# A hybrid encoder layer on Trainium2: left operands of the FFN's second Strassen half on GpSimd's queue, splits issued in two parts, RG-LRU's splits in an earlier slot

## The chip, the cores and the metric

The kernel runs on one core of one Trainium2 chip. The metric is the device time of one execution in microseconds (us), as the median of several runs.

## The reference

One encoder layer for two groups of tokens, a prompt of 1024 and a sample of 512, with shared weights and D = 1024; all arithmetic is float32. Cut to what matters:

```
h   = rmsnorm(x) * (1 + sc1) + sh1
z   = h @ w_in                       # rnn_x, rnn_gate, q, k, v, merge gates
xc  = conv4(rnn_x)
r,i = sigmoid(xc @ wa + ba), sigmoid(xc @ wx + bx)      # 16 blocks of 64, two directions
a   = exp(-8 r softplus(-lam));  u = sqrt(1 - a*a) * i * xc
rec = scan_forward(a, u) + scan_backward(a, u)          # RG-LRU
x   = x + gt1 * (merge(rec * gelu(gate), attention(q, k, v)) @ w_out)
h2  = rmsnorm(x) * (1 + sc2) + sh2
ff  = (silu(h2 @ w_g) * (h2 @ w_u)) @ w_ffn_out         # w_ffn_out: 2816 x 1024
y   = rmsnorm(x + gt2 * ff) * final_g
```

## The kernel before, in words

Every float32 product is made of three matmuls: an operand is split into a first part (rounded to the matmul's type, a ScalarE cast) and a second part (what is left, a VectorE subtraction), and first x first, first x second and second x first are added in PSUM. The helper `split` (L148 to L150) does cast and subtraction one behind the other. The order of all work is written out by hand: each engine runs its instructions in program order, DMA queues included, and only data and buffers make one engine wait for another.

**RG-LRU** (140 to 530 us). For each of eight column blocks j, TensorE makes one tile of `rnn_x` and one of the gate, each in six half groups of 12 matmuls of 512 columns. After every half group one slot of side work is taken from a list. `first` puts the six gates of a block (`gate`, L527 to L535: six matmuls into two of the four PSUM banks of the pool `sd`, then two ScalarE sigmoids that free them) into six slots; `second` (L600) puts the rest there: `exps` (X), the convolution of the next block (C), the two decays (E, three VectorE operations each), the split of the next block's `xc` (CS, L518 and L519), the split of its gate weights (`gw_split`, L499 and L500), the roots (Q, L558 and L559, two ScalarE operations each, of which one needs the decay), a scan (S) and Gelu (GE).

**FFN, second Strassen half** (from 2521 us). `w_ffn_out` is cut into 2 x 2 blocks, and seven products replace eight. Each product has six left operands (pairs of 128-token tiles), so there are 42 steps n. A step is 11 slices k of three matmuls with 512 columns (`mms`, L1600 to L1604), first parts first; even steps write the PSUM tile `mm` and read `a0hi`, `a0lo`, odd ones `sd` and `a1hi`, `a1lo`.

- `aload(n)` (L1285 to L1299) loads the left operand of step n, 128 x 1408 float32 or 704 KB, from `ffd` or `ffx` into one of two raw buffers (`araw`, seen as `slot` for even n and `wol` for odd); in two of the products it loads two of them. It is an SP DMA.
- `aprep(n, i)` (L1301) prepares part i of three of it: where there are two operands a VectorE sum (L1315, `asum`), then `split` into `acmb`. Two such pairs exist, so the parts of step n + 2 may be written only when TensorE is done with the same part of step n.
- `bbuild` (L1265) makes the right operand's slices for the next product, 11 in six steps: one or two loads of 256 KB from `w_fo` (`bload`, L1263, SP, two raw buffers `wo`; the load for slice n + 2 waits until slice n is split), a VectorE sum or difference (L1274) where there are two, and `split`.
- `take` (L1570) adds the finished product to the accumulators `acc` (L1526), `x1load` (L1534, SP) fetches the residual, `squares` (L1540, L1541 and L1543) adds it and sums the squares.

In the loop over the steps (L1625) the helpers stand at fixed slices k:

```python
if k == 1 and n: aprep(n + 1, 2); aload(n + 2)
elif k == 2: take(n - 1), x1load
elif k in (3, 6): bbuild(...)
elif k == 4: aprep(n + 2, 0)
elif k == 8: aprep(n + 2, 1)
elif k == 9 and done: squares(...)
```

Of the kernel before, what the change touches and what calls it, by code (L numbers as in the profile page):

```python
# [14 lines left out]
ALU = mybir.AluOpType  # L15
# [8 lines left out]
CH = 512  # L24
# [27 lines left out]
def encoder_kernel(  # L52
# [5 lines left out]
    v, s, g_, pe, sp = nc.vector, nc.scalar, nc.gpsimd, nc.tensor, nc.sync  # L58
# [55 lines left out]
    class Stream:  # L114
# [13 lines left out]
        def split(self, n, eng=v):  # L128
            self.load(n)
            while self.ns < min(n, len(self.srcs)):  # L130
                t = self.raws.pop(self.ns)
                hi = self.pool.tile(self.shape, F32R, tag=self.tags[1], name="whi")
                lo = self.pool.tile(self.shape, F32R, tag=self.tags[2], name="wlo")
                split(t, hi, lo, eng)
                self.parts[self.ns] = (hi, lo)
                self.ns += 1
# [299 lines left out]
    with ExitStack() as sc:  # L436
# [58 lines left out]
        def gw_split(j):  # L495
            a = graw.pop(j)
            for b, h in enumerate(hs):
                hi, lo = (w[h, :, 64 * b:64 * b + 64] for w in gws[j % 2])
                s.copy(out=hi, in_=a[h])  # L499
                v.tensor_tensor(out=lo, in0=a[h], in1=hi.bitcast(F32), op=ALU.subtract)  # L500
# [85 lines left out]
        def slots(*fs):  # L586

            for f in fs:
                side.append(lambda f=f: [a() for a in f])
# [10 lines left out]
        def second(p, c, j):  # L600

            C, CS = ([c["C"]], [c["CS"]]) if c else ([], [])
            gs = [lambda: gw_split(j)] if c else []
            if p:
                slots([p["X"]] + C + [p["E"][0]], [p["E"][1]], CS + [p["Q"][0]], gs + [p["Q"][1]], [p["S"][0]], [p["GE"]])
            else:
                slots(C, gs, CS, [], [], [])

# [5 lines left out]
        p = pp = None  # L614
        for j in range(KD):
# [9 lines left out]
            p, pp = cur, p  # L625
# [495 lines left out]
    def f32(a):  # L1121
        return a.bitcast(F32)
# [110 lines left out]
    KH = NFF // 2  # L1233
    AH = KH * P
# [14 lines left out]
    araw = [f32(slot[i][:, :2 * AH]) for i in (4, 3)]  # L1249
# [4 lines left out]
    def bload(upto):  # L1254

        while nbl[0] < min(upto, len(PRODO) * KH):
            q, k = divmod(nbl[0], KH)
            t = braw[nbl[0]] = wts.tile([P, D], F32, tag="raw", name="wo2")
            nbl[0] += 1
            for e, nm in enumerate(PRODO[q][2][:2]):  # L1260
                if nm:
                    i, j = int(nm[0]) - 1, int(nm[1]) - 1
                    sp.dma_start(out=t[:, e * CH:(e + 1) * CH], in_=w_fo[KH * i + k, :, j * CH:(j + 1) * CH])  # L1263

    def bbuild(upto):  # L1265

        while nbb[0] < min(upto, len(PRODO) * KH):
            n = nbb[0]
            bload(n + 1)
            nbb[0] += 1  # L1270
            t, r = braw.pop(n), bslot[n % 20]
            op = PRODO[n // KH][2][2]
            if op is not None:
                v.tensor_tensor(out=t[:, :CH], in0=t[:, :CH], in1=t[:, CH:], op=op)  # L1274
            split(t[:, :CH], r[:, :CH], r[:, CH:])
            bload(n + 3)

    def asrc(nm, i):
        t = PAIRS[i]
        if nm in ("d0", "d1", "s"):  # L1280
            return ffx[i, {"d0": 0, "d1": 1, "s": 2}[nm]]
        b = int(nm[1]) - 1
        return ffd[t + (3 if nm[0] == "2" else 0), :, b * AH:(b + 1) * AH]

    def aload(n):  # L1285

        if n >= NSTEP:
            return
        q, i = divmod(n, len(PAIRS))
        if n == 0:  # L1290
            a0["raw"] = upper
            for nm in ("hi", "lo"):
                a0[nm] = [wts.tile([P, D], F32R, tag=nm, name="a0" + nm) for _ in range(2)]
            bslot.extend(a0["hi"] + a0["lo"])
            for e, (o, w) in enumerate(((0, D), (D, AH - D))):
                sp.dma_start(out=a0["raw"][e][:, :w], in_=asrc("11", 0)[:, o:o + w])
            return
        for e, nm in enumerate(PRODO[q][1]):
            sp.dma_start(out=araw[n % 2][:, e * AH:(e + 1) * AH], in_=asrc(nm, i))  # L1299

    def aprep(n, i):  # L1301

        if n >= NSTEP:
            return
        c = slice(CH * i, min(CH * (i + 1), AH))
        w = c.stop - c.start
        if n == 0:
            e, o = divmod(CH * i, D)
            split(*(a0[nm][e][:, o:o + w] for nm in ("raw", "hi", "lo")))
            return  # L1310
        a, (hi, lo) = araw[n % 2], acmb[n % 2]
        t = a[:, c]
        if len(PRODO[n // len(PAIRS)][1]) == 2:
            t = tmp.tile([P, CH], F32, tag="t2", name="asum")[:, :w]
            v.tensor_tensor(out=t, in0=a[:, c], in1=a[:, AH + c.start:AH + c.stop], op=ALU.add)  # L1315
        split(t, hi[:, c], lo[:, c])

    def apart(n, k):
        if n:
# [4 lines left out]
    def column(p):  # L1324

        return p % NFF // 2 + NFF // 2 * (p % 2)
# [60 lines left out]
    with ExitStack() as sc:  # L1387
# [54 lines left out]
        for m, (p, c) in enumerate(order):  # L1442
# [3 lines left out]
            X, Y, u2, r = TX[p % 2], TX[2 + p % 2], TX[4 + p % 2], TX[6 + p % 2]  # L1446
            i, t0 = column(p), p // NFF * 6
# [65 lines left out]
    with ExitStack() as sc:  # L1513
# [16 lines left out]
        def x1load(t, f):  # L1530
            e, m = divmod(nx[0] % 4, 2)
            nx[0] += 1
            a = upper[e][:, m * CH:(m + 1) * CH]
            sp.dma_start(out=a, in_=x1d[t * P:(t + 1) * P, f])  # L1534
            return a

        def squares(t, f, xo, ps):

            a = acc[t][:, f]
            v.tensor_tensor(out=a, in0=a, in1=gt2[t // 8][:, f], op=ALU.mult)  # L1540
            v.tensor_tensor(out=a, in0=a, in1=xo, op=ALU.add)  # L1541
            e = f.start // CH
            s.activation(out=ps, in_=a, func=AF.Square, accum_out=st[:, 2 * t + e:2 * t + e + 1])  # L1543
# [56 lines left out]
        def mms(ps, n, k, cols=slice(0, CH)):  # L1600
            hi, lo, bh, bl = operands(n, k)
            pe.matmul(ps, lhsT=hi, rhs=bh[:, cols], start=k == 0, stop=False)
            pe.matmul(ps, lhsT=hi, rhs=bl[:, cols], start=False, stop=False)
            pe.matmul(ps, lhsT=lo, rhs=bh[:, cols], start=False, stop=k == KH - 1)  # L1604
# [4 lines left out]
        for n, k, f in (  # L1609
# [7 lines left out]
        ):  # L1617
            late[n, k] = f

        ps = None  # L1620
        tl = PAIRS[-1]
        for i in range(3):
            aprep(1, i)
        aload(2)
        for n in range(NSTEP - 1):  # L1625
            q, i = divmod(n, len(PAIRS))
            before, ps = ps, (sdb if n % 2 else mmb)()
            done = xo = None
            for k in range(KH):
                mms(ps, n, k)  # L1630
                if k == 1 and n:
                    aprep(n + 1, 2)
                    aload(n + 2)
                elif k == 2:
                    if n:
                        done = take(n - 1, before)
                    if q == 3 or done and done[1] is F2 and done[0] in PAIRS:
                        done = (PAIRS[i], F2) if q == 3 else None
                    if done:
                        xo = x1load(*done)  # L1640
                elif k in (3, 6):
                    t = (q + 1) * KH + (2, 4, 6, 8, 9, 11)[i]
                    bbuild(t - 1 if k == 3 else t)
                elif k == 4:
                    aprep(n + 2, 0)
                elif k == 8:
                    aprep(n + 2, 1)
                    if n == 0:
                        sp.dma_start(out=fgb, in_=final_g.partition_broadcast(P))
                        for e in range(2):  # L1650
                            src = gtd[1, e:e + 1, :].partition_broadcast(P)
                            sp.dma_start(out=gt2[e], in_=src.rearrange("p a d -> p (a d)"))
                elif k == 9 and done:
                    squares(*done, xo, before)
                if (n, k) in late:
                    late[n, k]()
            if n == NSTEP - 3:
                xl = x1load(tl, F1)
            if n == NSTEP - 2:

                a = acc[tl]
                v.tensor_tensor(out=a[:, F1], in0=a[:, F1], in1=gt2[1][:, F1], op=ALU.mult)
                v.tensor_tensor(out=a[:, F1], in0=a[:, F1], in1=xl, op=ALU.add)
                v.tensor_tensor(out=a[:, F2], in0=a[:, F2], in1=fgb[:, F2], op=ALU.mult)

        n = NSTEP - 1
        b = wts.tile([P, CH], F32, tag="raw", name="b")
        for e, pl in enumerate((sdb(), mmb())):
            cols = slice(256 * e, 256 * e + 256)
            pl = pl[:, cols]  # L1670
            for k in range(KH):
                mms(pl, n, k, cols)
                if e == 0 and k == 1:
                    late[n, 0]()
                    done = take(n - 1, ps)
# [11 lines left out]
            if e == 0:  # L1687
                v.tensor_tensor(out=st[:, 2 * tl:2 * tl + 1], in0=st[:, 60:61], in1=st[:, 2 * tl + 1:2 * tl + 2],
                                op=ALU.add)
# [3 lines left out]
        r = rs[:, tl:tl + 1]  # L1693
# [90 lines left out]
```

## Time and profile before

| | us |
|---|---|
| median of 3 runs | 2963.2 (2961.89 to 2963.86) |
| the profiled execution | 2960.41 |
| its span in the trace | 2958.6 |
| TensorE matmuls busy | 2832.6 (96%) |
| TensorE weight loads busy | 2351.5 (79%) |
| VectorE busy | 1927.5 (65%) |
| ScalarE busy | 1217.0 (41%) |
| GpSimd busy | 238.0 (8%) |

Engines are named PE (matmuls), PEld (weight loads), DVE (VectorE), ACT (ScalarE), POOL (GpSimd) and SP. L with a number is a line of the kernel before. The times of the rows are microseconds from the start of the span, and matmuls overlap: one of 512 columns is shown as 0.39 us, while the next starts 0.23 us after it. What follows "<-" in brackets is what ended the idle time before an instruction.

### The profile page before, as it was taken

How to read it: one execution, taken by the hardware profiler on the slowest of the kernel's cores; microseconds unless marked ns; L12 is line 12 of the kernel's file. 1: busy time of each engine (PE TensorE's matmuls, PEld its weight loads, DVE VectorE, ACT ScalarE, POOL GpSimd, SP SyncE). 2: the span in 40 equal slices, each digit the busy share in tenths (PEclk: the TensorE clock that was granted, in tenths of full speed). 3: DMA queues.
4: the chain of work that ended last, by engine and by line, in shares of the span. 5: the costliest groups of instructions: out<-in, count | busy, mean ns of one | idle time of the engine just before them, and what ended most of it. 6: DMA issues, size and time to landing. Idle time of an engine off the chain costs nothing. (4 is left out here: it accounts for less than half of the span.)

```text
span 2958.6 us, 38256 instructions
## 1 busy us (share of the span) xinstructions
PE 2832.6 (96%) x14165; PEld 2351.5 (79%) x14165; DVE 1927.5 (65%) x3615; ACT 1217.0 (41%) x2384; POOL 238.0 (8%) x312
## 2 busy tenths in 40 slices
PE   8999999999999999999999999999999999879887
PEld 5878777877777777777787777999999999667665
DVE  6486867455555555542758656898889887456667
ACT  6375757233333333335330145544444443333332
POOL 0000000000000000001523412011000000000001
PEclk9999999999999999999999999999999999899998
DMA  5211011110111011112677644675454443655555
GB/s 231 72 35 57 32 65 55 61 33 33 33 34 40 33 33 34 34 47 65 196 252 254 214 151 136 201 209 171 132 172 128 117 121 119 214 187 196 185 191 183
DMA packets 184395, 351.55 MB, mean 119 GB/s; under 512 B 20264, under 2 KB 99496, under 8 KB 183952
## 3 DMA queue, kind: packets, MB, share of 16 engines
q1 hardware_dynamic: 167648, 292.42, 30.8%
q0 software_dynamic: 16416, 56.42, 5.5%
q8 instruction: 111, 1.82, 0.3%
q14 instruction: 76, 0.62, 0.1%
q10 hardware_dynamic: 144, 0.26, 0.0%
HBM read 264.19 MB, written 84.85 MB: 118 GB/s over the span
## 5 line engine op out<-in xcount | busy, mean ns | idle before, releaser
L159 PE MATMUL mm<-hh,whi 128*128 128x512 f32 x1632 | 664.2, 407 | 2.0 <-DVE hh L292 1.5
L161 PE MATMUL mm<-hh,wlo 128*128 128x512 f32 x1632 | 642.4, 394 | 0.0
L160 PE MATMUL mm<-hl,whi 128*128 128x512 f32 x1632 | 641.5, 393 | 0.5 <-DVE hl L293 0.4
L159 PEld LDWEIGHTS mm<-hh,whi 128*128 128x128 f32 x1632 | 312.3, 191 | 71.1 <-issue 7.2
L161 PEld LDWEIGHTS mm<-hh,wlo 128*128 128x128 f32 x1632 | 308.7, 189 | 68.8
L160 PEld LDWEIGHTS mm<-hl,whi 128*128 128x128 f32 x1632 | 309.8, 190 | 62.8 <-DVE hl L293 3.3
L150 DVE TENSOR_TENSOR wlo<-wraw,whi 128x1024 fp32r<-128x1024 f32 x94 | 115.0, 1229 | 193.2 <-ACT whi L149 193.1
L747 ACT ACTIVATE sm<-sm,sg 128x192 f32<-128x192 f32 (+2 forms) x288 | 114.3, 398 | 303.5 <-DVE sg L742 303.0
L149 ACT CAST whi<-wraw 128x1024 fp32r<-128x1024 f32 x96 | 96.3, 1006 | 198.2 <-PE mm L160 86.2
L1361 DVE TENSOR_TENSOR sum<-wf 128x512 f32<-128x512 f32 x220 | 158.4, 720 | 1.5
L1363 ACT CAST woh<-sum 128x512 fp32r<-128x512 f32 x148 | 91.9, 622 | 153.2 <-DVE sum L1361 149.8
L742 DVE CUSTOM_DVE_ANT_0 sm<-sd,mk 128x192 f32<-128x192 f32 (+2 forms) x288 | 72.9, 291 | 117.0 <-PE sd L735 64.3
L668 DVE SCALAR_TENSOR_TENSOR t<-mm,rp 128x512 f32<-128x512 f32 x72 | 49.8, 692 | 150.3 <-PE mm L161 150.3
L1432 PE MATMUL mm<-top,woh 128*128 128x384 f32 x348 | 116.6, 335 | 3.2 <-DVE flat L1465 3.2
L1434 PE MATMUL mm<-top,woh 128*128 128x384 f32 x348 | 116.3, 334 | 0.0
L1433 PE MATMUL mm<-top,woh 128*128 128x384 f32 x348 | 116.3, 334 | 0.0
L1345 DVE TENSOR_TENSOR woh<-sum,woh 128x512 fp32r<-128x512 f32 x148 | 101.2, 684 | 0.6 <-ACT woh L1363 0.5
L857 DVE CUSTOM_DVE_ANT_0 jk<-ada 128x1024 bf16<-128x1024 f32 x64 | 81.4, 1285 | 22.8 <-DMA ada<-in_w_ada_dram 14.3
L1568 POOL DMA_DIRECT2D out_dram<-acc x22 | 12.0, 545 | 896.4 <-DVE acc L1567 895.0
L1434 PE MATMUL sd<-top,woh 128*128 128x384 f32 x240 | 80.2, 334 | 0.0
L1432 PE MATMUL sd<-top,woh 128*128 128x384 f32 x240 | 80.2, 334 | 0.0
L1433 PE MATMUL sd<-top,woh 128*128 128x384 f32 x240 | 80.2, 334 | 0.0
(446 smaller groups left out, 6465.4 us busy)
## 6 DMA issues: line engine op xcount, KB each, us to landing
wf<-in_w_fi_dram SPq DMA_DIRECT2D x88, 512.0 KB, 3.8
wraw<-in_w_in_dram SPq DMA_DIRECT2D x68, 512.0 KB, 3.5
wo<-in_w_fo_dram SPq DMA_DIRECT2D x132, 256.0 KB, 3.2
ffd<-flat SPq DMA_DIRECT2D x88, 192.0 KB, 3.7
ada<-in_w_ada_dram SPq DMA_DIRECT2D x32, 512.0 KB, 4.2
ffx<-flat SPq DMA_DIRECT2D x66, 192.0 KB, 2.5
wol<-ffd SPq DMA_DIRECT2D x18, 704.0 KB, 4.9
gated<-gs POOLq DMA_DIRECT2D x48, 256.0 KB, 2.6
```

What stands on the lines that cost most here:

```text
L149: s.copy(out=hi, in_=t)
L150: eng.tensor_tensor(out=lo, in0=t, in1=hi.bitcast(F32), op=ALU.subtract)
L159: pe.matmul(ps, lhsT=hi(k), rhs=xh(k), start=a, stop=False)
L160: pe.matmul(ps, lhsT=hi(k), rhs=xl(k), start=False, stop=False)
L161: pe.matmul(ps, lhsT=lo(k), rhs=xh(k), start=False, stop=z)
L747: s.activation(out=sm[:, c], in_=sm[:, c], func=AF.Exp, scale=-1.0, bias=sg[:, u, x:x + 1], accum_out=sg[:, u, x + 1:x + 2])
L1345: v.tensor_tensor(out=r[:, CH:], in0=t, in1=f32(r[:, :CH]), op=ALU.subtract)
L1361: v.tensor_tensor(out=t, in0=wraws[p, a], in1=wraws[p, b], op=op)
L1363: s.copy(out=r[:, :CH], in_=t)
L1432: pe.matmul(ps, lhsT=hi, rhs=bh[:, k], start=k == 0 and not more, stop=False, skip_group_check=more)
L1433: pe.matmul(ps, lhsT=hi, rhs=bl[:, k], start=False, stop=False, skip_group_check=more)
L1434: pe.matmul(ps, lhsT=lo, rhs=bh[:, k], start=False, stop=k == 3, skip_group_check=more)
```

## The change

Three things are moved; no arithmetic is added or taken away.

1. `aload` is issued on GpSimd's queue (except for step 0), and a step earlier: `aload(n + 3)` in step n behind slice 1, when the last part of step n + 1 has been split, which now stands behind slice 0.
2. `bbuild` and `aprep` take a list. With it they issue only the cast, and append the subtraction (with the next `bload`) to the list; the loop issues what is in the list at later slices (`flush`). Slices for `take`, `bbuild` and the second `aprep` are one earlier.
3. In RG-LRU's `second`, the splits of `xc` and the gate weights come ahead of the second decay.

```diff
             if p:
-                slots([p["X"]] + C + [p["E"][0]], [p["E"][1]], CS + [p["Q"][0]], gs + [p["Q"][1]], [p["S"][0]], [p["GE"]])
+                slots([p["X"]] + C + [p["E"][0]], CS + gs + [p["Q"][0]], [p["E"][1]], [p["Q"][1]], [p["S"][0]], [p["GE"]])
...
-            split(t[:, :CH], r[:, :CH], r[:, CH:])
-            bload(n + 3)
+            s.copy(out=r[:, :CH], in_=t[:, :CH])
+
+            def low(n=n, t=t, r=r):
+                v.tensor_tensor(out=r[:, CH:], in0=t[:, :CH], in1=f32(r[:, :CH]), op=ALU.subtract)
+                bload(n + 3)
+            if later is None:
+                low()
+            else:
+                later.append(low)
...
-            sp.dma_start(out=araw[n % 2][:, e * AH:(e + 1) * AH], in_=asrc(nm, i))
+            g_.dma_start(out=araw[n % 2][:, e * AH:(e + 1) * AH], in_=asrc(nm, i))
...
-        split(t, hi[:, c], lo[:, c])
+        s.copy(out=hi[:, c], in_=t)
+
+        def low():
+            v.tensor_tensor(out=lo[:, c], in0=t, in1=f32(hi[:, c]), op=ALU.subtract)
+        if later is None:
+            low()
+        else:
+            later.append(low)
...
+        lows = []
+
+        def flush(fs=None):
+            for f in list(lows if fs is None else fs):
+                lows.remove(f)
+                f()
+
         ps = None
         tl = PAIRS[-1]
+        aload(2)
         for i in range(3):
-            aprep(1, i)
-        aload(2)
+            aprep(1, i, lows)
+            if i:
+                flush(lows[:1])
+        flush()
...
                 mms(ps, n, k)
-                if k == 1 and n:
-                    aprep(n + 1, 2)
-                    aload(n + 2)
-                elif k == 2:
+                if k == 0 and n:
+                    aprep(n + 1, 2, lows)
+                elif k == 1:
                     if n:
                         done = take(n - 1, before)
...
+                    flush()
+                    aload(n + 3)
+                elif k in (2, 5):
+                    t = (q + 1) * KH + (2, 4, 6, 8, 9, 11)[i]
+                    had = list(lows)
+                    bbuild(t - 1 if k == 2 else t, lows)
+                    flush(had)
                 elif k in (3, 6):
-                    t = (q + 1) * KH + (2, 4, 6, 8, 9, 11)[i]
-                    bbuild(t - 1 if k == 3 else t)
+                    flush()
                 elif k == 4:
-                    aprep(n + 2, 0)
-                elif k == 8:
-                    aprep(n + 2, 1)
+                    aprep(n + 2, 0, lows)
+                elif k == 7:
+                    aprep(n + 2, 1, lows)
...
-                elif k == 9 and done:
-                    squares(*done, xo, before)
+                elif k == 9:
+                    flush()
+                    if done:
+                        squares(*done, xo, before)
```

How this moves instructions, at three places. First, SP's queue around step 21 of the FFN's second half, before (`wo` are the right operand's raw buffers, `wol` and `slot` with `ffx` the left operand's, with `x1d` the residual's):

```order
L1263 DMA wo_20813<-in_w_fo_dram 128x512 x2
L1263 DMA wo_20830<-in_w_fo_dram 128x512 x2
L1299 DMA wol<-ffx 128x1408
L1534 DMA slot<-x1d 128x512
L1263 DMA wo_20872<-in_w_fo_dram 128x512 x2
L1263 DMA wo_20889<-in_w_fo_dram 128x512 x2
```

and after the change:

```order
L1263 DMA wo_20814<-in_w_fo_dram 128x512 x2
L1263 DMA wo_20831<-in_w_fo_dram 128x512 x2
L1548 DMA slot<-x1d 128x512
L1263 DMA wo_20873<-in_w_fo_dram 128x512 x2
L1263 DMA wo_20890<-in_w_fo_dram 128x512 x2
```

The left operand's load is gone from between the right operand's loads. On GpSimd's queue these loads now follow one another with nothing between them until the output's stores.

Second, VectorE in step 21, before (L1526 is `take`, L150 the second part of a split, L1274 the right operand's sum, L1540 and L1541 `squares`):

```order
L150 TENSOR_TENSOR a0lo<-slot,a0hi 128x384
L1526 TENSOR_TENSOR acc_19646<-acc_19646,mm 128x512
L1274 TENSOR_TENSOR wo_20813<-wo_20813 128x512
L150 TENSOR_TENSOR woh<-wo_20813,woh 128x512
L150 TENSOR_TENSOR a1lo<-wol,a1hi 128x512
L1274 TENSOR_TENSOR wo_20830<-wo_20830 128x512
L150 TENSOR_TENSOR woh<-wo_20830,woh 128x512
L150 TENSOR_TENSOR a1lo<-wol,a1hi 128x512
L1540 TENSOR_TENSOR acc_19647<-acc_19647,gt_19654 128x512
L1541 TENSOR_TENSOR acc_19647<-acc_19647,slot 128x512
```

and after:

```order
L1540 TENSOR_TENSOR acc_19646<-acc_19646,mm 128x512
L1326 TENSOR_TENSOR a0lo<-slot,a0hi 128x384
L1274 TENSOR_TENSOR wo_20814<-wo_20814 128x512
L1278 TENSOR_TENSOR woh<-wo_20814,woh 128x512
L1274 TENSOR_TENSOR wo_20831<-wo_20831 128x512
L1326 TENSOR_TENSOR a1lo<-wol,a1hi 128x512
L1278 TENSOR_TENSOR woh<-wo_20831,woh 128x512
L1326 TENSOR_TENSOR a1lo<-wol,a1hi 128x512
L1554 TENSOR_TENSOR acc_19647<-acc_19647,gt_19654 128x512
L1555 TENSOR_TENSOR acc_19647<-acc_19647,slot 128x512
```

The same ten operations stand there; the second sum of the right operand has moved ahead of a second part of the left one, and `take` ahead of the other.

Third, VectorE in RG-LRU, the first block with a block ahead of it (`xs` is the split of `xc`, `glo` the second part of the gate weights; L550 to L552 a decay, L565 the scan):

```order
 L552 TENSOR_TENSOR i_997<-i_997,xc 128x1536
+L519 TENSOR_TENSOR xs_1177<-xc,xs_1176 128x1536
+L500 TENSOR_TENSOR glo_764<-graw,ghi_763 64x4x64 x2
 L550 SCALAR_TENSOR_TENSOR a_1148<-a_1148,r_1067 128x1536
 L551 SCALAR_TENSOR_TENSOR r_1067<-a_1148 128x1536
 L552 TENSOR_TENSOR i_1068<-i_1068,xc 128x1536
-L519 TENSOR_TENSOR xs_1193<-xc,xs_1192 128x1536
-L500 TENSOR_TENSOR glo_764<-graw,ghi_763 64x4x64 x2
 L565 TENSOR_TENSOR i_997<-i_997,r_996 128x1536
```

The two second parts have moved ahead of the second decay's three operations.

## Rows read from the trace of the kernel before

**Rows 1.** The page's part 2: granted TensorE clock in 40 slices, in tenths.

```profile
PEclk9999999999999999999999999999999999899998
```

**Rows 2.** Timeline of PE: step 2, a wait inside step 6, steps 39 and 40.

```profile
2544.14 0.39 PE L1602 MATMUL mm<-slot,a0hi 128*128 128x512 f32 x1
...
2606.67 0.80 PE L1602 MATMUL mm<-slot,a0hi 128*128 128x512 f32 x1 [6.63 <-ACT slot L149]
...
2919.43 0.39 PE L1602 MATMUL sd<-woh,a1hi 128*128 128x512 f32 x1
...
2926.91 0.39 PE L1602 MATMUL mm<-woh,a0hi 128*128 128x512 f32 x1
```

**Rows 3.** Windows: length, busy time and count by engine, PEclk, DMA share, GB/s.

```profile
140.00:500.00 360.00, 344.82 (x1439) 277.57 (x1438) 267.32 (x211) 240.32 (x248) 8.05 (x31) 0.96 0.14 47
2520.00:2525.00 5.00, 5.00 (x24) 4.05 (x24) 3.03 (x6) 2.18 (x4) 0.00 (x0) 1.00 0.90 327
2544.14:2926.91 382.77, 322.12 (x1256) 241.95 (x1254) 221.32 (x369) 127.44 (x248) 4.39 (x8) 0.94 0.57 194
2826.43:2889.61 63.18, 52.02 (x198) 38.12 (x198) 37.90 (x61) 20.41 (x41) 0.00 (x0) 0.95 0.55 185
```

**Rows 4.** Chain of waits in order of time, one loop, near step 9.

```profile
2623.37 0.70 DVE asum L1315
...
2624.18 0.63 ACT a1hi L149
...
2625.44 0.70 DVE woh L150
2626.15 0.33 SPq L1263
...
2626.53 0.43 SPq L1299
...
2627.01 5.61 DMA slot<-ffd
```

**Rows 5.** Waits of PE, 2521 to 2943 us: sum, times, longest.

```profile
PE mm L1602 <- ACT a0hi L149: 21.0, 13, 4.3
```

**Rows 6.** DMAs: GpSimd's store of `r` (ns; landing in us), SP's `wo` loads.

```profile
L581 POOL DMA_DIRECT2D rnnd<-r x8: 534/540/551, 181.1 to 531.4; - x8
...
DMA to landing us min/median/max: 3.5/3.6/6.0
...
wo<-in_w_fo_dram SPq DMA_DIRECT2D x108, 256.0 KB, 3.1
```

**Rows 7.** Waits of PE, 140 to 500 us.

```profile
PE sd L533 <- DVE xs L519: 12.3, 5, 2.5
PE sd L532 <- ACT ghi L499: 2.6, 5, 0.5
```

**Rows 8.** Timeline of DVE in RG-LRU, one block.

```profile
157.43 1.75 DVE L550 SCALAR_TENSOR_TENSOR a<-a,r 128x1536 f32<-128x1536 f32 x1
...
162.56 1.75 DVE L519 TENSOR_TENSOR xs<-xc,xs 128x1536 fp32r<-128x1536 f32 x1
164.23 0.86 DVE L500 TENSOR_TENSOR glo<-graw,ghi 64x256 fp32r<-64x256 f32 x2
165.13 1.76 DVE L565 TENSOR_TENSOR i<-i,r 128x1536 f32<-128x1536 f32 x1
```

**Rows 9.** Timeline of ACT, the same block.

```profile
161.39 1.49 ACT L558 ACTIVATE a<-a 128x1536 f32<-128x1536 f32 x1
...
167.42 1.03 ACT L149 CAST whi<-wraw 128x1024 fp32r<-128x1024 f32 x1
...
169.77 0.69 ACT L535 ACTIVATE r<-sd,gb 128x512 f32<-128x512 f32 x1
```

**Rows 10.** Timeline of PE, the first gate of the same block.

```profile
161.42 0.49 PE L532 MATMUL sd<-xs,ghi 128*128 128x512 f32 x1 [0.52 <-ACT ghi L499]
164.37 0.76 PE L533 MATMUL sd<-xs,ghi 128*128 128x512 f32 x1 [2.45 <-DVE xs L519]
```

More of the change, by code (lines that the diff above doesn't have):

```diff
@@ L1263, in bload, with bbuild @@
                     sp.dma_start(out=t[:, e * CH:(e + 1) * CH], in_=w_fo[KH * i + k, :, j * CH:(j + 1) * CH])
-    def bbuild(upto):
+    def bbuild(upto, later=None):
         while nbb[0] < min(upto, len(PRODO) * KH):
@@ L1298, in aload, with aprep @@
         for e, nm in enumerate(PRODO[q][1]):
-            sp.dma_start(out=araw[n % 2][:, e * AH:(e + 1) * AH], in_=asrc(nm, i))
-    def aprep(n, i):
+            g_.dma_start(out=araw[n % 2][:, e * AH:(e + 1) * AH], in_=asrc(nm, i))
+    def aprep(n, i, later=None):
         if n >= NSTEP:
```

## The prediction, made before the changed kernel ran

> **What bounds the kernel now.** I read the page's forty slices first, then the stretches that lose TensorE time, then the chain of waits there. In the slices the granted clock stays at nine tenths or more except in the last fifth, where slices show eight [rows 1]. That fifth is the second Strassen half of the FFN: 42 steps of 33 matmuls of 512 columns. Its pace can be read from two neighbouring steps without a wait: they start 7.48 us apart [rows 2], so one matmul takes 7.48/33 = 0.2267 us when nothing is late. But from the start of step 2 (2544.14) to the start of step 40 (2926.91) the 38 steps take 382.77 us, 10.07 us each. Two kinds of loss make up the difference: TensorE stands still, for instance 6.63 us inside step 6 [rows 2], and after standing still it runs partly at the lower of its two clock levels, so that the granted clock over these steps is 0.94 of full speed [rows 3]. VectorE is busy for 221 of the 383 us, the DMA engines for 0.57 of it, so no engine is full.
>
> The chain of waits shows what is late [rows 4]. It is a closed loop of 9.3 us per step (2623.37 to 2627.01 + 5.61): the left operand's rows land (5.61 us), VectorE adds the two pieces, ScalarE casts the first part, VectorE then finishes the right operand's second part (the `woh` in the chain), and that frees a raw buffer for which SP has waited with the next load of `w_fo` (L1263). Only behind it in the same queue stands the next left operand's load (L1299), and its 5.6 us begin. In the program the load for step n+2 is issued after the second product slice of step n, and its first split stands three slices later, 2 us; the transfer takes 5.6. So VectorE, ScalarE and SP fall back until the whole loop sets the pace. TensorE's longest wait there, in sum, is for the first parts of the left operand: 21.0 us in the even steps alone [rows 5].
>
> The second place is RG-LRU. Between 140 and 500 us TensorE waits five times for the splits of `xc`, 12.3 us for the second part and 2.6 for the gate weights' [rows 7], and the clock is at 0.96 there [rows 3].
>
> **The change, part by part.**
>
> Left operands. The load for step n+3 is now issued in step n behind slice 1, on GpSimd's queue, and its first split stands behind slice 4 of step n+1: 1 step and 3 slices, 7.48 + 3 x 0.68 = 9.5 us later, and the product that needs it starts another step and 7 slices after that. The buffer it fills is free by then, because the last split of step n+1 was moved ahead of it. The transfer's 5.6 us [rows 4] therefore lie beside matmuls. Cover: more than 9.5 us; were it gone, the old loop of 9.3 us would be back. Each issue costs GpSimd 0.54 us [rows 6], and it does nothing else there until the output stores of the last product. GpSimd's queue has not carried this transfer before; nearest is its store of 128 x 1536 f32, 768 KB, which lands in 3.6 us in the median and 6.0 at most [rows 6], and I take 4 to 6 us. Where a step has two operands it is two such loads; the DMA engines have carried 327 GB/s over 5 us [rows 3], and the same 194 GB/s squeezed into 7.48 instead of 10.07 us make 261, so they fit.
>
> The Trainium skill, page "DMA: Bandwidth & Descriptors", sections "Specifications" and "Issuing engine by pattern", speaks against this move: simple loads belong on SyncE, and a first byte takes about 1 us by GpSimd's software path against 0.6 by the hardware's. By it an estimate of 42 x 0.4 = 17 us would be given back if the loads still ended the wait; the rows show them covered, and GpSimd's 768 KB no slower than SP's 704 KB.
>
> SP's queue loses 53 loads of 704 KB (5 for the first product, 12 each for the two with two left operands, 24 for the last four). What is left are the `w_fo` loads and `x1d`, in order. A right operand's buffer is used once per step: add 0.70, cast 0.63, second part 0.69, issues 0.33 + 0.43, landing 3.1 [rows 4, 6], together 5.9 us, below 7.48.
>
> First and second parts apart. Between a sum and its second part VectorE waited 0.74 us for ScalarE's cast (the sum ends at 2624.07, the cast at 2624.81 [rows 4]); now other work stands in most of these places. Work is neither added nor removed. In the heaviest product it is 37.9 us for six steps [rows 3], and six steps at full pace are 44.9: 84%, so it does not become the bound. I cost the move at nothing by itself.
>
> So steps 2 to 39 go from 382.77 us to 38 x 7.48 = 284.24: **-98.5 us**. This includes the clock, since nothing stands still. The bounds: if every step still lost 0.5 us, -79.5; more than -98.5 is not possible. The first two steps I leave as they are: their waits are for the end of the first half (the last right operand and the split of step 1), whose code and order are the same. The end, 31.69 us from the start of step 40 to the span's end, is norm, scaling and stores on VectorE, and I leave it too (-2 to 0).
>
> RG-LRU. The split of `xc` and of the gate weights (1.75 and 0.86 us on VectorE) now stands ahead of the second decay [rows 8]. It would start at 157.43 instead of 162.56 and end at 160.0, and TensorE comes to the first gate at 161.42 - 0.52 = 160.90 [rows 10], so both waits go. What is late next: the second decay moves back by 2.57 us (162.56 to 165.13). Its second operation then ends near 163.5, and ScalarE's second root (L558), which started at 161.39, needs that; with it Gelu, a weight cast and the gate's sigmoids move back by 2.2 us, since they follow on ScalarE without a gap [rows 9]. The gates use four PSUM banks, two each. The third gate needs the first one's banks, and TensorE reaches it 36 matmuls after the first, at 160.90 + 8.16 = 169.06. The sigmoid that frees the bank ended at 169.77 + 0.69 and now ends near 172.6: a wait of 3.5 us in place of one of 0.52 and one of 2.45. Five times 3.5 is 17.7 against 15.2 idle now, and the clock falls after one as after the other. I take **0** for this part. Its bounds: everything gained, 15.2 idle and half of 8% of 360 us, 14.4, at the lower clock: -30; or the longer wait with a longer fall of clock, +10.
>
> The sum: 2958.6 - 98.5 + 0 = 2860.1 span; the profiled execution took 2960.4, so 2861.9, and the median of the runs is 2.8 above it: **2865**.
>
> **The rivals.**
>
> 1. The right operands become the bound. More traffic makes the `w_fo` loads slower than 3.1 us. There are 11 builds in six steps for two buffers, so a buffer may take 44.9/5.5 = 8.16 us, which is reached when a load lands in 5.3 us. At 6.3 us a product of six steps takes 50.4 instead of 44.9, in the four products that build with two operands, 22 us, less one step of slack: about 2880. For it: 261 GB/s on average, in bursts. Against: the loads of 704 KB no longer stand in the same queue.
>
> 2. RG-LRU gains in full. If the sigmoids come early enough, or the banks are freed otherwise than I read it, up to 30 us more go: 2835. For it: both waits named in the rows are removed. Against: ScalarE's chain without a gap [rows 9].
>
> 3. Slower than before. GpSimd's loads land so late that two buffers do not cover them: two steps last as long as a landing plus the 8 of 11 slices from first to last split, so the pace is landing/1.27. It passes 10.07 us when a load takes 12.8 us; at 14 us steps take 11.0, and 38 x 0.95 = 36 us make 3000. For it: in this stretch the queue has not carried loads before. Against: 3.6 and 6.0 us [rows 6]. It would also be the case in which the change does not do what it says.
>
> **How the numbers follow.** Forecast 0.60 (2858 to 2872), rival 1 0.17 (2872 to 2890), rival 2 0.18 (2832 to 2857), rival 3 0.04; 0.01 is left for a gain that cancels. The range takes most of rivals 1 and 2: 2835 to 2888. Faster by over 0.2% (about what a measurement of this kernel can tell from no change): 0.95; within: 0.01; slower: 0.04.
>
> **What would show it.** In the changed profile steps 2 to 40 start 7.48 us apart with a granted clock of 0.99 or 1.00, VectorE waits for no left operand's DMA, and SP's chain L1263, L1299 is gone. In RG-LRU the wait of L533 for `xs` is gone and L532 waits for ScalarE's sigmoid (L535) five times, some 3.5 us each. I am wrong about RG-LRU if that wait is missing, and about the FFN if steps keep a pace above 7.7 us.

## The result, and the profile after

The changed kernel took **2865.16 us** in the median of four runs (2862.92 to 2867.15), the kernel before beside it 2962.55 (2957.75 to 2963.86). The ratio is 0.9674, with a 95% interval from 0.9657 to 0.9691. The profiled execution took 2862.92 us, its span is 2861.0: 97.6 less than the 2958.6 of before.

I read the second half of the FFN first. On the timeline of PE, step 2 starts at 2537.95 and step 40 at 2825.48 [rows 2 has 2544.14 and 2926.91]; between them there are three waits of over 0.2 us:

```profile
2537.95 0.39 PE L1616 MATMUL mm<-slot,a0hi 128*128 128x512 f32 x1
...
2621.28 0.50 PE L1616 MATMUL mm<-wol,a0hi 128*128 128x512 f32 x1 [1.11 <-ACT wol L1275]
2622.09 0.50 PE L1617 MATMUL mm<-wol,a0hi 128*128 128x512 f32 x1 [0.31 <-DVE wol L1278]
...
2825.48 0.39 PE L1616 MATMUL mm<-woh,a0hi 128*128 128x512 f32 x1
```

The third, 0.22 us, lies in step 24. The long wait of 6.63 us in step 6 is gone. The windows of RG-LRU, of steps 2 to 39 and of the end (columns as in [rows 3]):

```profile
140.00:500.00 360.00, 342.66 (x1459) 278.69 (x1458) 272.38 (x214) 242.50 (x252) 8.03 (x31) 0.98 0.14 47
2537.95:2825.48 287.53, 285.85 (x1255) 234.98 (x1254) 215.84 (x362) 123.05 (x243) 30.18 (x57) 1.00 0.75 252
2825.48:2861.00 35.52, 15.56 (x100) 14.06 (x98) 26.47 (x72) 6.46 (x19) 7.57 (x14) 0.75 0.35 131
```

The 38 steps take 287.53 us instead of 382.77, at a granted clock of 1.00 instead of 0.94: TensorE is busy for 285.85 of them, and VectorE's work is about what it was (216 us, before 221). In RG-LRU the clock is 0.98 instead of 0.96, and the two waits of [rows 7] are one:

```profile
PE sd L532 <- ACT r L535: 17.3, 5, 3.5
```

So the 97.6 us come from three places: 95.2 in steps 2 to 39, 6.2 by which step 2 starts earlier, and 3.8 that the end takes longer, 35.52 us in place of 31.69 from step 40's start to the span's end.

What is new is that VectorE trails TensorE. Before, VectorE and ScalarE waited 85.8 us for loads of left operands in steps 2 to 39 (sum, times, longest):

```profile
DVE asum L1315 <- DMA slot<-ffd: 17.3, 6, 8.7
DVE asum L1315 <- DMA wol<-ffd: 12.4, 6, 4.0
ACT a1hi L149 <- DMA wol<-ffd: 20.4, 4, 9.4
ACT a0hi L149 <- DMA slot<-ffx: 16.5, 8, 4.3
ACT a1hi L149 <- DMA wol<-ffx: 14.4, 8, 4.2
ACT a0hi L149 <- DMA slot<-ffd: 4.8, 2, 3.8
```

After the change ScalarE waits 3.4 us for them and VectorE 2.7, once. Most of VectorE's waiting is now for ScalarE, as its longest waits show:

```profile
DVE a1lo L1326 <- ACT a1hi L1323: 12.2, 17, 1.1
DVE a0lo L1326 <- ACT a0hi L1323: 11.3, 15, 1.1
DVE wo L1274 <- DMA wo<-in_w_fo_dram: 11.0, 6, 6.3
DVE acc L1540 <- ACT acc L1599: 10.1, 6, 1.7
DVE acc L1540 <- ACT acc L1593: 6.9, 6, 1.1
...
DVE asum L1322 <- DMA slot<-ffd: 2.7, 1, 2.7
```

The 6.3 us for a load of `w_fo` lie in step 3, and the 2.7 us for a left operand in steps 4 and 5; TensorE has no wait in steps 2 to 11. L1593 and L1599 are the copies in `take`. In the second product VectorE's steps are 8.09 us apart (the second part of the last third of a left operand starts at 2586.49, 2594.57 and 2602.66), so it loses 0.6 us to TensorE in each; in the fourth it is 8.73. The lead holds this back until the first steps of the products behind, steps 12 and 24, where the right operand is late.

### The profile page after: what moved, and what is told of

It reads as the page before. It is cut to its first block, busy times and chain, and to the rows that moved or that the text cites. A ratio compares the mean times of both kernels' runs of the same rounds, so it can differ in the third digit from the quotient of the medians.

```text
span 2861.0 us, 38290 instructions
## 1 busy us (share of the span) xinstructions
PE 2787.7 (97%) x14165; PEld 2340.4 (82%) x14165; DVE 1925.6 (67%) x3615; ACT 1212.4 (42%) x2384; POOL 266.0 (9%) x365
## 5 line engine op out<-in xcount | busy, mean ns | idle before, releaser
L150 DVE TENSOR_TENSOR wlo<-wraw,whi 128x1024 fp32r<-128x1024 f32 x94 | 115.5, 1235 | 196.2 <-ACT whi L149 196.1
L161 PE MATMUL mm<-rh,wlo 128*128 128x512 f32 x192 | 75.2, 392 | 3.8 <-DVE wlo L150 3.8
```

The costliest lines, as they stand in the source:

```text
L150: eng.tensor_tensor(out=lo, in0=t, in1=hi.bitcast(F32), op=ALU.subtract)
L161: pe.matmul(ps, lhsT=lo(k), rhs=xh(k), start=False, stop=z)
```

## The experiments

My theory after the result: the loads issued early enough are what counts, the queue and the separate first and second parts are not. Its rivals: GpSimd's queue does it, or the separate parts do. Two further questions were what RG-LRU's part is worth, and what made the end longer. Line numbers of an experiment can be off by a few from those of the changed kernel; those of `one_word` are those of before.

### ffn_only and rg_only: one half of the change each

```diff
 # ffn_only: the changed kernel with
-slots([p["X"]] + C + [p["E"][0]], CS + gs + [p["Q"][0]], [p["E"][1]], [p["Q"][1]], ...)
+slots([p["X"]] + C + [p["E"][0]], [p["E"][1]], CS + [p["Q"][0]], gs + [p["Q"][1]], ...)
 # rg_only: the kernel before with the opposite edit
```

> The changed kernel with RG-LRU's table of slots as it was before (the splits behind the second decay); the FFN's part stays. Theory: the two parts are independent, and RG-LRU's is worth the 4.7 us by which its last gate comes earlier in the changed kernel's trace: 2870 us (2867 to 2874); TensorE waits five times some 2.5 us for xs at L533 and about 0.5 us for the gate weights, and steps 2 to 39 of the FFN's second half take 287 to 288 us. Rival: the 4.7 us are given back further on, and RG-LRU's part is worth nothing: 2865 us (2863 to 2867).

> The kernel before with RG-LRU's new table alone. Theory: one wait takes the place of two, five times 3.5 us at L532 for the sigmoid (L535) in place of 0.5 and 2.5 us, and a little of the clock comes back: 4 to 7 us faster than before, 2957 us (2954 to 2960). Rival: the FFN's closed loop takes the gain, no change: 2962 us. Second rival: all the idle time and the clock come back, 2930 us.

`ffn_only` took 2869.94 us (ratio to before 0.969, 0.9675 to 0.9705), `rg_only` 2960.51 against 2962.93 (ratio 0.9991, 0.9979 to 1.0003). The first lies on the theory's figure, but its interval overlaps that of the changed kernel; the second can't be told from no change, where I had expected 4 to 7 us. The waits are as expected in both. In `rg_only`:

```profile
PE sd L532 <- ACT r L535: 17.4, 5, 3.5
```

and in `ffn_only`:

```profile
PE sd L533 <- DVE xs L519: 12.3, 5, 2.5
PE sd L532 <- ACT ghi L499: 2.5, 5, 0.5
```

The trace tells the size better. From TensorE's coming to the first gate of this stretch (the wait there counted in) to the last gate it is 332.7 to 332.9 us in the three traces with the old table (before, `ffn_only`, `one_word`), and 330.1 in the mean of the eight with the new one (327.2 to 331.9). RG-LRU's part is worth 2 to 3 us; the 4.7 that I read from the changed kernel's one trace were in part scatter.

### sp_queue and no_lead: the queue or the lead

```diff
 # sp_queue: the changed kernel with
-            g_.dma_start(out=araw[n % 2][:, e * AH:(e + 1) * AH], in_=asrc(nm, i))
+            sp.dma_start(out=araw[n % 2][:, e * AH:(e + 1) * AH], in_=asrc(nm, i))
 # no_lead: the changed kernel with
-        aload(2)
...
-                    aload(n + 3)
+                    aload(n + 2)
```

> The changed kernel with the left operands' loads back on SP's queue, still a step ahead. Theory: the lead does it, not the queue: the load lands in 5 to 6 us and has over 9 us in either queue, steps 2 to 39 take 285 to 293 us, 2865 us (2860 to 2875). Rival: SP's queue is the bound, since a left operand's load stands behind a w_fo load that waits for its buffer and holds up the next one itself: over 8.2 us a step, 2895 us or more.

> The changed kernel with the loads on GpSimd's queue but without the step of lead: behind slice 1 of step n the load for step n+2 in place of n+3, its first split three slices (2 us) later as in the kernel before. Theory: the lead does it; VectorE stands for the load in each step (landing 5 to 6 us, then add, cast and the rest of its own work of a step, some 4 to 5 us), so 9.5 to 10.5 us a step and 2955 us (2935 to 2975). Rival: the queue does it, since the load no longer stands behind the w_fo loads: 7.5 to 8 us a step, 2866 to 2885 us.

`sp_queue` took 2862.26 us (0.9648 to 0.9678): the same as the changed kernel or a little better, with 287.51 us in steps 2 to 39. GpSimd's queue is not needed. The landing of the left operands (medians by buffer and source, of which the trace of `sp_queue` gives three) is 4.2 to 5.4 us there, 4.5 to 5.8 in the changed kernel.

`no_lead` took 2885.98 us (0.9734 to 0.9771), and my expectation for the lead failed: I had 2955. Its windows, steps 2 to 35 and steps 36 to 39:

```profile
2541.87:2797.48 255.61, 255.08 (x1124) 210.47 (x1122) 190.27 (x312) 111.97 (x217) 23.74 (x45) 1.00 0.76 257
2797.48:2839.81 42.33, 33.11 (x134) 25.28 (x132) 21.44 (x45) 9.94 (x23) 4.88 (x9) 0.92 0.44 143
```

34 steps run at 7.52 us each, although the load stands a step later in the program. The timeline of POOL in this run shows why, and why the last steps are slow:

```profile
2603.35 1.05 POOL L1306 DMA_DIRECT2D slot<-ffd  x2 [7.03 <-DVE asum L1322]
2611.44 1.05 POOL L1306 DMA_DIRECT2D wol<-ffd  x2 [7.04 <-DVE asum L1322]
...
2807.48 1.22 POOL L1582 DMA_DIRECT2D out_dram<-acc  x2 [13.36 <-DVE acc L1581]
2808.68 0.54 POOL L1306 DMA_DIRECT2D slot<-ffx  x1
2818.73 1.21 POOL L1582 DMA_DIRECT2D out_dram<-acc  x2 [9.51 <-DVE acc L1581]
2819.99 0.54 POOL L1306 DMA_DIRECT2D wol<-ffx  x1
```

GpSimd has nothing ahead of the load, so it stands at it for 7 us until its buffer is read (the last sum, L1322), and issues it at once: 1.64 us into step 10, whose start is at 2601.71. In the changed kernel the load of the same step waits for its buffer in the same way, and goes out 3.42 us into step 10 (start 2597.79), no earlier:

```profile
2601.21 1.05 POOL L1306 DMA_DIRECT2D slot<-ffd  x2 [7.03 <-DVE asum L1322]
```

So the edit took away no lead there. Only in the last product are output stores (L1582) ahead of it, which wait for VectorE; the loads of steps 38 to 41 come late behind them, and TensorE waits up to 5.4 us:

```profile
PE mm L1616 <- ACT a0hi L1323: 7.7, 2, 5.4
```

So the run showed that what counts is when the load is free to be issued, and that either a place further ahead or an empty queue gives this.

### one_word: the empty queue alone

```diff
 # the kernel before with
-            sp.dma_start(out=araw[n % 2][:, e * AH:(e + 1) * AH], in_=asrc(nm, i))
+            g_.dma_start(out=araw[n % 2][:, e * AH:(e + 1) * AH], in_=asrc(nm, i))
```

> The kernel before with the left operands' loads on GpSimd's queue and nothing else changed. Theory (an empty queue gives the lead by itself): GpSimd has nothing ahead of the load but the wait for its buffer, which comes free a step earlier than the place where the load stands; so the load is issued as early as with the lead, only VectorE's standing for casts is left as in the run joined, and at the very end the loads queue behind the output stores as in the run no_lead: 2890 to 2915 us. Rival: the place in the program decides when a load is issued, and without the lead the loop of 9 to 10 us a step stays: 2950 us or more.

2910.78 us against 2963.58 (ratio 0.9817, 0.9802 to 0.9832): 53 us from the engine that issues the load, with no step of lead in the program. Steps 2 to 35 (269.49 us) and steps 36 to 39, the latter behind the stores again:

```profile
2545.91:2815.40 269.49, 262.53 (x1123) 211.02 (x1122) 188.28 (x306) 108.87 (x213) 23.70 (x45) 0.99 0.71 240
2815.40:2862.52 47.12, 34.73 (x133) 25.04 (x132) 23.38 (x50) 12.56 (x27) 4.87 (x9) 0.95 0.45 144
```

The Trainium skill, page "Trainium Kernel Development and Optimization", section "Key Constraints", says that issuing from several engines only saves the sequencer's issue time, as all transfers share the same DMA engines. By it 53 issues of 0.43 us [rows 4], 23 us of SP's own time, would be saved and little more; the run shows 53 us of the kernel's. What it saved is the time in which the load stood in SP's order behind a `w_fo` load that waited for VectorE.

### joined and apart_only: first and second parts

```diff
 # joined: the changed kernel, in bbuild and in aprep, with
-            if later is None:
-                low()
-            else:
-                later.append(low)
+            low()
 # apart_only: the changed kernel with the edits of sp_queue and of no_lead together
```

> The changed kernel with every second part issued right behind its cast again (both operands); queue and lead stay. Prediction's theory: the move is worth nothing by itself, since VectorE has 16% to spare: 2865 us (2862 to 2870). Rival: VectorE stands 0.74 us for each cast, three of the left operand and on average 11/6 of the right one, 3.6 us a step on top of 5.8 us of work (221 us in 38 steps): 9.4 us a step, the pace of the old loop, whatever the loads do: 38 x 1.9 = 72 us, 2937 us (2905 to 2950), with VectorE without a gap but for the casts.

> The changed kernel with first and second parts issued apart and RG-LRU's new table, but the left operands' loads on SP's queue and for step n+2, as before. Theory of the lead: VectorE and ScalarE stand for the load in each step, SP holds the next one behind the w_fo loads, and the loop keeps 9 us or more a step: 2925 us or more. Rival, that the parts issued apart do it: VectorE no longer stands for casts, the loop gets shorter by some 2 to 3 us and fits into 7.48 us in most steps: 2865 to 2890 us.

`joined` took 2886.05 us (0.9722 to 0.9757), 21 us more than the changed kernel: between the two theories, and not nothing. `apart_only` took 2937.35 (0.9895 to 0.9931): the separate parts alone don't make the loop fit. The windows of steps 2 to 39 in `joined`:

```profile
2543.88:2853.36 309.48, 296.36 (x1256) 236.37 (x1254) 216.45 (x362) 123.58 (x244) 30.18 (x57) 0.98 0.71 236
```

and in `apart_only`:

```profile
2542.67:2907.17 364.50, 317.22 (x1256) 241.25 (x1254) 219.18 (x368) 124.58 (x246) 4.38 (x8) 0.95 0.60 203
```

Together with before and after this is a square (us for steps 2 to 39):

| | loads late on SP | loads early on GpSimd |
|---|---|---|
| parts joined | 382.77 (before) | 309.48 (`joined`) |
| parts apart | 364.50 (`apart_only`) | 287.53 (after) |

Early loads are worth 73 to 77 us, separate parts 18 to 22, and they nearly add up (73.3 + 18.3 = 91.6 of the 95.2). The lead alone, with the loads on SP's queue both times, gives 77.0 us as well (364.50 in `apart_only`, 287.51 in `sp_queue`). The kernel before also has `take`, `bbuild` and the second `aprep` one slice later than the other three, and no run moves these places alone. They gain nothing by themselves: `one_word` and `joined` both have the loads early and the parts joined, and steps 2 to 35 take 269.49 us with the old places and 273.16 with the new.

Where the parts are joined VectorE waits for more casts (steps 2 to 39 of `joined`):

```profile
DVE a1lo L1323 <- ACT a1hi L1320: 24.6, 28, 1.2
DVE a0lo L1323 <- ACT a0hi L1320: 22.8, 27, 1.2
DVE woh L1278 <- ACT woh L1275: 11.0, 16, 0.7
```

against 12.2 and 11.3 for the left operands after the change, and what it falls back by then reaches TensorE as late right operands. I had expected up to 72 us for this, from 3.6 us of waiting in each step. With the shorter rows of this view VectorE waits for 98 casts in 38 steps, 77 us or 2.0 us a step (38 us in all after the change); my rival had counted nearly five a step.

### take: VectorE's add ahead of ScalarE's copy

```diff
 # the changed kernel, second product (and likewise the fourth)
-                s.copy(out=acc[t1][:, F1], in_=ps)
-                add(t2, F2, ps)
+                add(t2, F2, ps)
+                s.copy(out=acc[t1][:, F1], in_=ps)
```

> The changed kernel where VectorE adds a product's result to the one half of an accumulator before ScalarE copies it to the other (second and fourth product). Theory: VectorE's waits for those copies (L1593 and L1599, 1.1 and 1.7 us in each of 12 steps, 17 us) go, it no longer falls back behind TensorE there, and the late right operands at steps 12 and 24 (1.1 + 0.3 and 0.2 us, and the clock behind them, some 3.3 us together) go as well: 2862 us (2859 to 2865). Rival: the lateness there comes from the loads of w_fo and not from VectorE: 2865 us, with the same waits.

2859.37 us (0.9634 to 0.9665). The interval just overlaps that of the changed kernel, but the trace is plain: VectorE's waits for the copies are gone, and of TensorE's at steps 12 and 24 none is left. Steps 2 to 39 take 285.31 us, 1.07 above 38 x 7.48:

```profile
2541.32:2826.63 285.31, 284.96 (x1255) 235.34 (x1254) 218.85 (x368) 125.36 (x246) 30.17 (x57) 1.00 0.76 256
```

The lateness was VectorE's, not that of the `w_fo` loads. The end, from step 40's start, is 30.6 us here.

### fin: the last scaling by GpSimd and ScalarE

```diff
 # the changed kernel, squares()
+            if t != tl:
+                g_.tensor_tensor(out=a, in0=a, in1=fgb[:, f], op=ALU.mult)
 # fin()
-                v.scalar_tensor_tensor(out=a[:, f], in0=a[:, f], scalar=r, in1=fgb[:, f], ...)
+                s.mul(out=a[:, f], in_=a[:, f], mul=r)
```

> The changed kernel with the last scaling taken from VectorE: the product with the final weights goes to GpSimd right behind the squares (11 tiles in two halves, 1.4 to 1.6 us each by its other rows of this size), the product with the row's factor to ScalarE. Theory: in the changed kernel's last 20 us, behind the last matmul, VectorE works off what it is late by, without a gap, and ten of these operations (7 us) lie in that queue behind the start of step 40; the lag of some 5 us in the last product goes too: 2855 us (2850 to 2860). Rival: GpSimd's products stand ahead of the last left operands' loads and the stores, or slow VectorE down, and what is gained is lost: 2865 us or more.

2874.44 us (0.9679 to 0.9717), slower than the changed kernel. The end became 3.3 us shorter (32.2 us), but steps 2 to 39 took 295.80. One of GpSimd's products, and then VectorE beside it:

```profile
2752.97 1.29 POOL L1559 TENSOR_TENSOR acc<-acc,fgb 128x512 f32<-128x512 f32 x1 [5.85 <-ACT mm L1557]
```

```profile
2752.04 1.28 DVE L1540 TENSOR_TENSOR acc<-acc,sd 128x512 f32<-128x512 f32 x2
2753.31 1.36 DVE L1326 TENSOR_TENSOR a1lo<-wol,a1hi 128x384 fp32r<-128x384 f32 x1
```

The second part that runs beside the product takes 1.36 us; in the changed kernel the same shape takes 0.56:

```profile
2782.85 0.56 DVE L1326 TENSOR_TENSOR a0lo<-slot,a0hi 128x384 fp32r<-128x384 f32 x1 [0.60 <-ACT a0hi L1323]
```

The same operation comes 8.44 us apart in these steps (2776.76, 2785.20, 2793.64), where the changed kernel has 7.65: VectorE loses 0.8 us to each of GpSimd's products, and the 0.74 us of scaling spared for it come only at the end. The Trainium skill, page "GPSIMD Engine Reference", sections "Specifications" and "Key points", says that GpSimd shares its SBUF interfaces with VectorE and contends with instructions that have two SBUF inputs; L1326 is one, and the trace agrees. The rival held.

### rg_order: the decays first, then the splits

```diff
 # the changed kernel; decay() keeps its first two operations, the product with xc becomes M
-slots([p["X"]] + C + [p["E"][0]], CS + gs + [p["Q"][0]], [p["E"][1]], [p["Q"][1]], [p["S"][0]], ...)
+slots([p["X"]] + C + p["E"], CS + gs + [p["Q"][0]], [p["M"][0], p["Q"][1]], [p["M"][1]], [p["S"][0]], ...)
```

> The changed kernel with another order of VectorE's work in RG-LRU: the two operations of each decay that the roots wait for come first, for both directions, then the splits of xc and of the gate weights, and only then the two products with xc (L552 of the kernel before). Theory: the wait that the change left is made by the second decay standing behind the splits; now its second operation ends near 159.1 us in place of 163.3, ScalarE's second root is not held up, the sigmoids come 3 us earlier, and the five waits of 3.5 us at L532 fall below 1 us, the second part of xc being ready near 160.9 us, just as TensorE comes to it: 13 to 15 us of waiting and 2 to 4 us of the clock's loss go, 2849 us (2845 to 2853). Rival: another engine's chain holds up TensorE there instead (the scans move back on VectorE by 1.7 us and with them the next weights' second part), 2860 us or more.

2848.90 us (ratio 0.9606, 0.9591 to 0.9621), on the theory's figure. The window of RG-LRU and TensorE's waits in it:

```profile
140.00:500.00 360.00, 355.99 (x1541) 287.94 (x1540) 287.73 (x224) 258.07 (x266) 10.18 (x35) 1.00 0.16 55
```

```profile
PE sd L532 <- ACT i L535: 2.6, 5, 0.5
PE sd L534 <- DVE glo L500: 1.4, 5, 0.3
```

The granted clock is 1.00, and from the first gate to the last it is 310.0 us instead of 330.1. VectorE's order in the same block as [rows 8]:

```profile
156.46 1.76 DVE L551 SCALAR_TENSOR_TENSOR r<-a 128x1536 f32<-128x1536 f32 x1
158.14 1.75 DVE L519 TENSOR_TENSOR xs<-xc,xs 128x1536 fp32r<-128x1536 f32 x1
```

The second decay's result is there at 158.2 us (L551), the second part of `xc` at 159.9. Both were possible at once; the change had only traded one for the other.

### best: the three edits that helped

```diff
 # the changed kernel with the edits of rg_order, take and sp_queue
```

> The changed kernel with three further edits together: RG-LRU's order as in the run rg_order, the accumulators' adds ahead of ScalarE's copies as in the run take, and the left operands' loads on SP's queue as in the run sp_queue. Theory: the three lie in different places; 15 to 17 us for RG-LRU, 5.8 us for the adds (2859.4 against 2865.2) and at most 3 us for the queue: 2842 us (2837 to 2848). Rival: in the FFN the two edits work against each other, SP's queue holding up the w_fo loads: 2850 us or more.

2840.21 us (2837.91 to 2841.01; ratio 0.9579, 0.9565 to 0.9593), faster than both kernels: 25 us below the changed one. Steps 2 to 39 are within 0.4 us of 38 x 7.48:

```profile
2519.91:2804.54 284.63, 284.59 (x1255) 235.28 (x1254) 219.39 (x369) 125.80 (x246) 4.37 (x8) 1.00 0.77 258
```

## Why the prediction came true, point by point

**The time** is 2865.16 against 2865 predicted, but the closeness is partly luck: three terms were off by 3 to 6 us and cancelled (-95.2, -6.2 and +3.8 in place of -98.5, 0 and 0).

**Steps 2 to 39: -98.5 predicted, -95.2 measured.** That nothing stands still and the clock comes back with it was right. The 3.3 us were lost at steps 12 and 24. I had reckoned VectorE at 84% of the pace, by its work alone, and so not the bound; with its waits for ScalarE its steps take 8.1 and 8.7 us in two products. `take` showed this by removing one kind of wait.

**"I cost the move at nothing by itself"** (first and second parts apart) failed: it is worth 18 to 22 us. The sum came out because I had set the steps to TensorE's own pace, 7.48 us, which no run here passed; it already held what the separate parts give, so a total that is right doesn't say that its parts are. With the rows that I had, 0.74 us of waiting for each cast, times five or so casts in a step, could have been set beside VectorE's 5.8 us of work; that would have been too much, as `joined` shows, but not nothing.

**"Were it gone, the old loop of 9.3 us would be back."** For the cover as I reckoned it, from the places in the program, this failed: in `no_lead` and `one_word` the places are late and the loop isn't back, since an otherwise empty queue issues a load when its buffer is free. The cover is not what I reckoned in the changed kernel either. The load for step 12 has its place behind slice 1 of step 9, near 2591.7, but its buffer is free and the load issued only at 2601.21, as VectorE trails. It is in time because VectorE's first sum from it comes late as well, 10.0 us after the issue:

```profile
2611.21 0.69 DVE L1322 TENSOR_TENSOR asum<-slot 128x512 f32<-128x512 f32 x1
```

That this is near the 9.5 us that I counted is luck. In `apart_only`, where the load is late in fact, most of the loop is back (9.6 us a step).

**The end: -2 to 0 predicted, +3.8 measured.** I had written that GpSimd does nothing else until the output stores of the last product, and did not follow it to the loads behind those stores. The changed kernel's timeline of POOL, and VectorE, which then stands for the cast:

```profile
2819.09 1.07 POOL L1582 DMA_DIRECT2D out_dram<-acc  x2 [6.65 <-DVE st L1573]
2820.15 0.54 POOL L1306 DMA_DIRECT2D wol<-ffx  x1
```

```profile
2827.39 0.69 DVE L1326 TENSOR_TENSOR a1lo<-wol,a1hi 128x512 fp32r<-128x512 f32 x1 [2.64 <-ACT a1hi L1323]
```

Step 41's load goes out behind two stores, and VectorE, which from here works almost without a gap to the end (three waits, 1.8 us together), loses 2.64 us. With the loads on SP's queue the end takes 32.0 us, with a VectorE that is less late 30.6.

**RG-LRU: 0 predicted; 2 to 3 us gained.** The wait that I forecast came at the place and in the size given (L532 for L535, five times, 3.5 us). What I took to cancel out did not quite: TensorE stands still for 2 us more than before, but the granted clock is 0.98 instead of 0.96. Of the signs that I had named, two came out not quite as named: steps 12 and 24 are longer than 7.48 us, and VectorE still waits for a left operand's DMA once (2.7 us).

**The rivals.** Right operands as the bound: their loads land in 4.2 us in place of 3.1, below the 5.3 that I gave as the point, and what lateness there was came from VectorE.

```profile
wo<-in_w_fo_dram SPq DMA_DIRECT2D x132, 256.0 KB, 4.2
```

RG-LRU in full: not by this change, but `rg_order` gained 16.3 us. Late loads by GpSimd: they land in 4.5 to 5.8 us, far from 12.8.

**What stays open:** where the rest of the 6.2 us ahead of step 2 arose. Step 2 starts at 2541.9 in the mean of the eight traces with the new table (2537.95 to 2545.11) and at 2545.1 in the three with the old one. That is 3.2 us, about what RG-LRU's table is worth. The other half of the 6.2 us is seen in the changed kernel's trace, the earliest of the eight, and not in their mean; what made it early is not shown.

## What to carry to other kernels

A load is issued when everything ahead of it on its queue has been issued and its own wait is over; so ask what it stands behind and when its buffer is free, not only where it stands in the program, and follow each queue to its end, where it may change its company. An engine is a bound by its work plus the waits for its neighbours that lie in its order: a cast on one engine and the rest on another are better issued with something between them. When a change moves one operation ahead of another and both are waited for, look for a third that neither wait needs, and move that one back.

## What the hardware showed that I had not expected

A product of 128x512 f32 on GpSimd (1.28 us) makes VectorE's second part beside it take 1.36 us in place of 0.56, 0.8 us lost for an operation that cost VectorE 0.74 us itself. And a load of 704 KB lands on GpSimd's queue about as soon as on SP's (4.5 to 5.8 against 4.2 to 5.4 us, both at some 250 GB/s in steps 2 to 39).
